# A mixer in another order: conv gate and value first, early low-priority taps, second queries ahead of attention

## The chip, the cores and the metric

The kernel runs on one core of one Trainium2 chip. The metric is the device time of one execution in microseconds (us). The core has five engines with a queue each: TensorE (PE in the profile), VectorE (DVE), ScalarE (ACT), GpSimd (POOL) and SyncE (SP), which issues nearly all transfers. Each engine takes its instructions strictly in the order in which they were put into its queue.

## The reference

Two layers of a diffusion backbone work on 640 tokens (512 latent, 128 context) of width 1024. A layer is a half-step feed-forward block, a mixer, and a second half-step feed-forward block. The change is in the mixer:

```python
h = _rms(x, p['norm_g'][1]) * (1.0 + sc2) + sh2
u = h @ p['w_in']                                   # 1536 columns: pool 256, conv 512, q 512, k 128, v 128
o_pool = _pool_mixer(u[..., :POOL_WIDTH], p['pool_w'], p['pool_scale'])
o_conv = _conv_mixer(u[..., POOL_WIDTH:ATTN_OFFSET], ...)
q, k, v = _qkv(u[..., ATTN_OFFSET:], p['q_norm_g'], p['k_norm_g'])
o_attn = ...            # 8 query heads, 2 key heads; banded latent attention plus cached context keys
x = x + g2 * (jnp.concatenate([o_pool, o_conv, o_attn], axis=-1) @ p['w_out'])

def _conv_mixer(g, dw, db, norm_g, pw):
    glu = g[..., :CONV_WIDTH] * jax.nn.sigmoid(g[..., CONV_WIDTH:])
    y = depthwise_conv(glu, dw, 31 taps, centred) + db
    return jax.nn.silu(_rms(y, norm_g)) @ pw
```

Queries and keys are normalised by head, latent ones are rotated by position (`rope`), and the softmax has a sink logit for each head.

## The kernel before, in words

Features lie on the 128 partitions and the 640 tokens along the free axis, in two halves of 320, one PSUM bank each. Products are done in fp32 by splitting both sides into a high and a low part and adding three products. A chunk of 128 output columns with 8 input blocks is 48 products of 128x128 by 320, and its weights are split by ScalarE (high) and VectorE (remainder, line 359).

`mixer` (line 784) builds the middle of a layer. `u_chunks` (line 796) makes two such chunks of the input projection for each of six names: `cg` (gate of the convolution), `ca` (its value), `kv` (keys and values), `q0` and `q1` (queries 0, 1 and 2, 3: each "query" tile holds two heads), and `pl` (pooling). `conv_gate` and `conv_value` make the gated input `glu`, one padded row of 688 for each of two channel blocks ("channels"). `conv_taps` (line 920) adds the 31 taps into `cy` (in the profile `cy<-glu,taps,cy` and `cy<-cy,cm`): those of channel 0 on VectorE (line 930); of channel 1 the first tap (line 928) and the last four on VectorE, and taps 1 to 26 as a product `cm` on ScalarE (line 933) and an add on GpSimd (line 934). The tag of these tiles has three buffers, two of which are the sums `cy`, so there is one `cm` at a time. `keys` (line 835) and `query_heads` (line 937) take the statistics of the heads, a Newton inverse root in short 128x10 steps on VectorE (lines 309 to 315), the rotation, whose two products are on GpSimd (lines 819 and 820), and the high and remainder copies `KS`, `KC` and `QS`.

Attention runs in 8 batches (`batch`, line 1057): for each of four query tiles the latent blocks 0 and 1, then 2, 3 and the context block. A batch is scores `a_*s` on TensorE, a masked maximum on VectorE (line 1083), short steps that end in `nm`, exponentials on ScalarE (line 1091), normalising copies (line 1095), transposes `a_*t` on TensorE through one PSUM bank, copies out of it on ScalarE (line 1099), and the product with the values, `a_*o` (line 1105). In the names, `a_3_2` is query tile 3, the batch that begins with block 2.

The output projection is done in two parts of four input blocks each. Part 0 (`out_chunks`, line 1111, products `p_0_m`, 24 for each of eight `m`) takes pooling and the first two attention tiles (`mix` 0, 1, 4, 5); part 1 (`last_group`, line 722, products `p_1_m_h` on line 743) takes the last two attention tiles and the convolution, and runs on into the next feed-forward block, whose row sums (`r_ss`, line 443) follow it.

What sets the order: the code states the work in one order, and a scheduler puts it on the engines' queues by priority, which follows the stated order; `high_priority(offset)` moves a piece forward (attention batches by 200) or, with a negative offset, back. The attention loop has 20 steps; tables say how much else is stated in each: `TAP_PLAN` the taps of each channel, `FILL` the modulation steps of the next block, `PLAN` the pieces of `background()` (`q1`, `pl`, then part 0), and `CONV_AT` the step from which the convolution's norm, gate and pointwise product (`convolution`) are stated. Tiles live in tagged pools; a new tile waits until the buffer it gets is read for the last time.

## Time and profile before

| | |
|---|---|
| median of 3 runs | 2480.34 us (2479.79 to 2483.69) |
| the profiled execution | 2478.26 us, span 2476.5 us |
| TensorE, VectorE, ScalarE, GpSimd busy | 95%, 69%, 41%, 19% of the span |
| first mixer | about 517 to 796 us |
| second mixer | about 1725 to 2007 us |

The page gives averages over a program in which feed-forward blocks take most of the time. The mixer is read from the busy times of single stretches and from the timeline of each engine. A timeline row is start, duration, engine, line, operation, output and inputs, shape and count; brackets at its end hold the engine's idle time before it and what ended it.

### The profile page before, as it was taken

Reading aid. Unit: us, or ns where it says so; the run is one execution under the profiler, and the core shown is the slowest. Engines: PE = TensorE matmul, PEld = TensorE weight load, DVE = VectorE, ACT = ScalarE, POOL = GpSimd, SP = SyncE. Lnnn points to the kernel's source line nnn. Section 1 sums busy time; section 2 is a strip of 40 time slices with the busy share of each in tenths; the row PEclk is TensorE's granted clock in tenths of the full one; section 3 lists DMA queues with packets and bytes.
Section 4 is the critical chain, followed back from the end, with each engine's and each line's share of the span. In section 5 each row is a group of like instructions: output and inputs, shape, how many; then the busy total and the mean of one; then the engine's idle time right before and its main releaser. Section 6 shows DMA issues by size and latency. Waiting matters only on the chain.

```text
span 2476.5 us, 40450 instructions
## 1 busy us (share of the span) xinstructions
PE 2348.3 (95%) x16491; PEld 2222.1 (90%) x16491; DVE 1707.3 (69%) x3174; ACT 1021.5 (41%) x1865; POOL 475.7 (19%) x376
## 2 busy tenths in 40 slices
PE   4999999999888899999989999999988889999999
PEld 4899999998568899999989999999975789999998
DVE  4667676667875876676669484858588569585855
ACT  2433333344674533333345242425266545242423
POOL 2101020121431211111132020212024323020210
PEclk7999999999998999999999999999998899999999
DMA  5444332222512123342312424223243022222222
GB/s 172 131 141 132 98 125 69 92 94 91 181 63 71 49 94 128 104 133 94 121 61 82 141 82 141 86 86 101 73 148 134 22 77 69 86 82 81 86 77 77
DMA packets 193990, 246.04 MB, mean 99 GB/s; under 512 B 5705, under 2 KB 176494, under 8 KB 193804
## 3 DMA queue, kind: packets, MB, share of 16 engines
q1 hardware_dynamic: 191824, 240.81, 29.9%
q8 instruction: 130, 2.13, 0.4%
q0 software_dynamic: 512, 1.95, 0.3%
q10 hardware_dynamic: 1468, 0.70, 0.1%
q14 instruction: 56, 0.46, 0.1%
HBM read 240.55 MB, written 2.88 MB: 98 GB/s over the span
## 4 chain that ended last, share of the span: by engine, by line
PE 82%; DVE 10%; ACT 4%; DMA 2%; issue 2%; SPq 0%; POOL 0%; ACTq 0%; DVEq 0%; POOLq 0%
PE f_B L555 11%; PE o_a L379 11%; PE f_C L555 11%; PE o_b L379 11%; PE f_A L555 11%; PE f_D L555 6%; PE f L596 3%; PE p L743 2%; PE mod L266 2%; PE o L743 1%; PE u_q_b L379 1%; PE u_q_a L379 1%; DVE cy L930 1%; DVE xa_l L397 1%; DVE X L421 1%
## 5 line engine op out<-in xcount | busy, mean ns | idle before, releaser
L379 PE MATMUL o_a<-f_h,o_wh 128*128 128x320 f32 x1344 | 402.9, 310 | 0.0
L379 PE MATMUL o_b<-f_h,o_wh 128*128 128x320 f32 x1344 | 401.4, 309 | 0.0
L421 DVE SCALAR_TENSOR_TENSOR X<-o_a,gate,X 128x320 f32<-128x320 f32 x120 | 65.8, 549 | 305.3 <-PE o_a L379 305.0
L379 PEld LDWEIGHTS o_a<-f_h,o_wh 128*128 128x128 f32 x1344 | 251.0, 188 | 8.7 <-ACT o_wh L358 5.8
L547 POOL TENSOR_TENSOR f_t<-f 128x512 f32<-128x512 f32 x80 | 127.6, 1595 | 660.1 <-DMA f<-in_ffn_wi_dram 556.0
L379 PEld LDWEIGHTS o_b<-f_h,o_wh 128*128 128x128 f32 x1344 | 251.4, 188 | 2.9 <-issue 2.9
L358 ACT ACTIVATE o_wh<-wo 128x768 fp32r<-128x768 f32 (+1 forms) x120 | 95.9, 800 | 381.0 <-PE o_b L379 259.7
L654 POOL TENSOR_TENSOR f_t<-f_t,f 128x512 f32<-128x512 f32 x80 | 114.4, 1430 | 638.1 <-DVE f_q_wl L533 332.8
L379 PE MATMUL o_b<-f_h,o_wl 128*128 128x320 f32 x672 | 207.3, 308 | 0.0
L379 PE MATMUL o_a<-f_h,o_wl 128*128 128x320 f32 x672 | 207.0, 308 | 0.0
L531 ACT ACTIVATE f_q_wh<-f_t 128x512 fp32r<-128x512 f32 x140 | 85.9, 629 | 199.5 <-DVE f_t L545 55.0
L379 PEld LDWEIGHTS o_b<-f_h,o_wl 128*128 128x128 f32 x672 | 126.2, 188 | 0.0
L379 PEld LDWEIGHTS o_a<-f_h,o_wl 128*128 128x128 f32 x672 | 126.0, 188 | 0.0
L359 DVE TENSOR_TENSOR o_wl<-wo,o_wh 128x768 fp32r<-128x768 f32 (+1 forms) x120 | 108.2, 903 | 15.6 <-ACT o_wh L358 15.0
L934 POOL TENSOR_TENSOR cy<-cy,cm 128x655 f32<-128x655 f32 x52 | 88.7, 1705 | 148.4 <-ACT cm L933 148.4
L531 ACT ACTIVATE f_P_wh<-f 128x512 fp32r<-128x512 f32 x112 | 66.5, 626 | 120.2 <-PE f_A L555 78.2
L555 PE MATMUL f_B<-F_h,f_q_wl 128*128 128x320 f32 x352 | 108.7, 309 | 0.8 <-DVE f_q_wl L533 0.8
L555 PE MATMUL f_B<-F_h,f_q_wh 128*128 128x320 f32 x352 | 108.7, 309 | 0.2 <-ACT f_q_wh L531 0.2
L555 PE MATMUL f_B<-F_l,f_q_wh 128*128 128x320 f32 x352 | 108.6, 308 | 0.0
L555 PE MATMUL f_C<-F_h,f_m_wh 128*128 128x320 f32 x336 | 103.6, 308 | 0.0
L555 PE MATMUL f_C<-F_l,f_m_wh 128*128 128x320 f32 x336 | 103.6, 308 | 0.0
L555 PE MATMUL f_C<-F_h,f_m_wl 128*128 128x320 f32 x336 | 103.5, 308 | 0.0
(541 smaller groups left out, 7349.9 us busy)
## 6 DMA issues: line engine op xcount, KB each, us to landing
f<-in_ffn_wi_dram SPq DMA_DIRECT2D x88, 1024.0 KB, 5.2
mw<-in_mod_w_dram SPq DMA_DIRECT2D x72, 1024.0 KB, 5.1
wo<-in_ffn_wo_dram SPq DMA_DIRECT2D x48, 768.0 KB, 4.9
wo<-in_ffn_wo_dram SPq DMA_DIRECT2D x16, 512.0 KB, 3.4
wout<-in_w_out_dram SPq DMA_DIRECT2D x32, 256.0 KB, 3.2
win_q<-in_w_in_dram SPq DMA_DIRECT2D x4, 1024.0 KB, 5.1
xt<-in_x_sample_dram SPq DMA_DIRECT2D x4, 512.0 KB, 5.5
win_cg<-in_w_in_dram SPq DMA_DIRECT2D x2, 1024.0 KB, 5.1
```

The source lines that it names most:

```text
L266: PE.matmul(ps[32 * g:32 * g + 32, 0:256], C[:, k, :], w[:, :, g, :], start=(k == 0), stop=(k == KD - 1))
L358: A.activation(out=wh, in_=src, func=AF.Copy)
L359: V.tensor_tensor(out=wl, in0=src, in1=wh.bitcast(F32), op=ALU.subtract)
L379: PE.matmul(ps[:, :n], ww[:, k, :], xx[:, lo:lo + n], start=(k == order[0] and i == 0), stop=(k == order[-1] and i == 2))
L421: V.scalar_tensor_tensor(out=X[:, m, s:e], in0=ps[:, s - o:e - o], scalar=gate[:, m, c:c + 1], in1=X[:, m, s:e], op0=ALU.mult, op1=ALU.add)
L531: A.activation(out=h, in_=src, func=AF.Copy, scale=sign)
L547: G.tensor_tensor(out=t3, in0=self.block(g, 1, 1), in1=self.block(g, 0, 1), op=ALU.add)
L555: PE.matmul(ps[:, :HALF], w[:, kp, :], self.F[f][kp][:, i, :], start=(first and kp == 0 and n == 0), stop=(kp == 3 and n == 2), skip_group ...
L596: PE.matmul(ps[:, :HALF], w[:, k, :], x, start=(k == 0 and n == 0), stop=(k == KD - 1 and n == 2))
L654: G.tensor_tensor(out=t2, in0=t2, in1=self.block(g, 1, 0), op=ALU.add)
L743: PE.matmul(ps[:, :HALF], w[:, m % 2, k, :], x[:, h * HALF:(h + 1) * HALF], start=(k == 0 and n == 0), stop=(k == 3 and n == 2))
L934: G.tensor_tensor(out=y, in0=y, in1=m, op=ALU.add)
```

## The change

The input projection is stated in the order gate, value, keys and values, queries 0, 1, and queries 2, 3 now follow ahead of the attention loop. Three taps of each channel are stated after each chunk of keys and values and of the queries, with a priority 250 lower than where they stand. In the loop each step has two taps of each channel, the convolution's norm begins at step 6 instead of 15, and `PLAN` is another. Part 0 of the output projection takes pooling and convolution, part 1 the four attention tiles. The normalised input `xa` gets a pool of its own, which is given up once the last chunk of the input projection has been stated; in its place stands a pool for tiles of pooling and convolution (two `mixp`, ten `part`) that were in the shared tags before.

```diff
-CONV_AT = 15
-TAP_PLAN = ((3, 2, 1, 2, 3, 2, 0, 2, 2, 1, 3, 2, 0, 2, 1, 3, 1, 1, 1, 3), (2, 4, 3, 3, 4, 4, 4, 2, 0, 4, 1, 1, 0, 1, 2, 1, 2, 0, 1, 4))
-ORDER, BEHIND = ("cg", "kv", "q0", "ca"), ("q1", "pl")
-PLAN = (0, 1, 0, 1, 0, 2, 0, 1, 0, 0, 0, 1, 1, 1, 2, 1, 1, 1, 1, 0)
+CONV_AT = 6
+TAP_EARLY, TAP_LATER = 3, 250
+TAP_PLAN = 2
+ORDER, BEHIND = ("cg", "ca", "kv", "q0"), ("q1", "pl")
+PLAN = (0, 1, 0, 1, 0, 1, 1, 0, 0, 0, 0, 0, 1, 1, 1, 1, 1, 1, 1, 1)
...
     def phase(name):
 
+        upper(None)
         if "cm" in scope:
...
+    def upper(name):
+
+        if "upper_cm" in scope:
+            scope.pop("upper_cm").__exit__(None, None, None)
+        if name:
+            cm = tc.tile_pool(name=name, bufs=1, reuse_waits="tile")
+            scope["upper_cm"], scope["upper"] = cm, cm.__enter__()
...
             catch_up()
+            upper(f"parts{l}")
             for c, (ph, pl) in enumerate(parts):
...
-                m = act([P, 2, T], F32R, f"mixp{l}{c}")
+                m = scope["upper"].tile([P, 2, T], F32R, tag="mixp", name=f"mixp{l}{c}", bufs=2)
...
+        def part(name, dt=F32R):
+            return scope["upper"].tile([P, T], dt, tag="part", name=name, bufs=10)
...
-                th = tmp(f"cth{l}{c}")
+                th = part(f"cth{l}{c}", F32)
...
-                mh, ml = tmp(f"mch{l}{c}", dt=F32R), tmp(f"mcl{l}{c}", dt=F32R)
+                mh, ml = part(f"mch{l}{c}"), part(f"mcl{l}{c}")
...
+        def early_taps():
+            with tc.high_priority(offset=-TAP_LATER):
+                for cc in range(2):
+                    conv_taps(cc, TAP_EARLY)
+
...
                 if k_steps and nm != "kv":
                     next(k_steps[0], None)
+                if nm in ("kv", "q0"):
+                    early_taps()
...
-            yield from out_chunks([0, 1, 4, 5], 0, lambda m: None)
+            yield from out_chunks([0, 1, 2, 3], 0, lambda m: None)
 
         bg = background()
+        for _ in range(2):
+            next(bg)
+            early_taps()
...
-                        conv_taps(cc, TAP_PLAN[cc][i], behind[cc])
+                        conv_taps(cc, TAP_PLAN, behind[cc])
...
-        for _ in conv:
-            next(bg, None)
+        assert next(conv, None) is None
...
-            for i, k in ((0, 6), (2, 2)):
+            for i, k in ((0, 4), (2, 6)):
...
-        return into_ffn(l, 2, ins["ffn2_wi"][l], f"p{l}_1", load, lambda k: mix[(6, 7, 2, 3)[k]], gate_of(l, 1, 1.0))
+        return into_ffn(l, 2, ins["ffn2_wi"][l], f"p{l}_1", load, lambda k: mix[4 + k], gate_of(l, 1, 1.0))
```

Three places in the resulting order. The first is VectorE's queue at the start of the keys' inverse root (`kv`, `rk_y` and `rk_w` are its 128x10 tiles, `u_kv_t` keys or values, `cy` the sum of channel 0, `u_q` the queries), before:

```order
L809 TENSOR_SCALAR u_kv_t<-u_kv_t,u_kv_b 128x128
L843 TENSOR_SCALAR kv_5495<-k_st 128x10
L309 TENSOR_SCALAR rk_y<-kv_5495 128x10
L312 TENSOR_TENSOR rk_w_5499<-rk_y 128x10
L313 SCALAR_TENSOR_TENSOR rk_w_5499<-rk_w_5499,kv_5495 128x10
L315 SCALAR_TENSOR_TENSOR rk_y_5502<-rk_w_5499,rk_y 128x10
L312 TENSOR_TENSOR rk_w_5504<-rk_y_5502 128x10
L313 SCALAR_TENSOR_TENSOR rk_w_5504<-rk_w_5504,kv_5495 128x10
```

and now:

```order
L940 SCALAR_TENSOR_TENSOR cy_5234<-glu_5427,taps,cy_5234 128x655 x3
L853 TENSOR_SCALAR kv_5652<-k_st 128x10
L940 SCALAR_TENSOR_TENSOR cy_5234<-glu_5427,taps,cy_5234 128x655
L319 TENSOR_SCALAR rk_y<-kv_5652 128x10
L940 SCALAR_TENSOR_TENSOR cy_5234<-glu_5427,taps,cy_5234 128x655
L322 TENSOR_TENSOR rk_w_5656<-rk_y 128x10
L425 TENSOR_TENSOR u_q_t<-u_q_a,r_5223 128x320
L323 SCALAR_TENSOR_TENSOR rk_w_5656<-rk_w_5656,kv_5652 128x10
L369 TENSOR_TENSOR u_q_wl<-win_q_5961,u_q_wh 128x1024
L325 SCALAR_TENSOR_TENSOR rk_y_5659<-rk_w_5656,rk_y 128x10
```

Taps of channel 0 and pieces of the queries' work stand ahead of and among the short steps, which followed one another before.

The second is GpSimd's queue at the first rotations (`qr_sh` and `u_q_t` of the queries, `kr_sh` and `u_kv_t` of the keys), before:

```order
L405 TENSOR_TENSOR xa_acc<-xa_acc,sq_7_5190 128x640
L819 TENSOR_TENSOR qr_sh<-qr_sh,tab_4900 128x512
L820 TENSOR_TENSOR u_q_t<-u_q_t,tab_4900 128x512
L819 TENSOR_TENSOR kr_sh<-kr_sh,tab_4900 128x512
L820 TENSOR_TENSOR u_kv_t<-u_kv_t,tab_4900 128x512
L907 MEMSET glu_5841 128x15 x3
```

and now (`cy_5235` is the sum of channel 1):

```order
L944 TENSOR_TENSOR cy_5235<-cy_5235,cm_5912 128x655
L944 TENSOR_TENSOR cy_5235<-cy_5235,cm_5915 128x655
L944 TENSOR_TENSOR cy_5235<-cy_5235,cm_6025 128x655
L829 TENSOR_TENSOR qr_sh<-qr_sh,tab_4903 128x512
L830 TENSOR_TENSOR u_q_t<-u_q_t,tab_4903 128x512
L944 TENSOR_TENSOR cy_5235<-cy_5235,cm_6028 128x655
L829 TENSOR_TENSOR kr_sh<-kr_sh,tab_4903 128x512
L830 TENSOR_TENSOR u_kv_t<-u_kv_t,tab_4903 128x512
L944 TENSOR_TENSOR cy_5235<-cy_5235,cm_6031 128x655
```

The rotations, which stood behind the squares of the norm, now stand behind and among adds of channel 1. Twelve such adds are ahead of the first rotation, 17 ahead of attention.

The third is TensorE's queue at the end of the last attention batch (`a_3_2t` its transposes, `a_3_2o` the product with the values, `rc_ss` the row sum of the convolution's norm), before:

```order
L1098 MATMUL a_3_2t_7507<-con,a_3_2S_7467 128x128 x4
L1098 MATMUL a_3_2t_7514<-con,a_3_2S_7472 128x128 x4
L1098 MATMUL a_3_2t_7521<-con,a_3_2S_7477 128x128 x3
L1098 MATMUL a_3_2t_7527<-con,a_3_2S_7482 128x128 x3
L1098 MATMUL a_3_2t_7533<-con,a_3_2S_7487 128x128
L1098 MATMUL a_3_2t_7537<-con,a_3_2S_7492 128x128
L323 MATMUL rc_ss<-ones,ca_7359 128x1 x5
L1105 MATMUL a_3_2o<-a_3_2S_7467,VS_5227 64x128
```

and now:

```order
L753 MATMUL p_1_0_0_7741<-mixa_6607,p_1_0_wh 128x320 x2
L753 MATMUL p_1_0_0_7741<-mixa_6607,p_1_0_wl 128x320
L753 MATMUL p_1_0_0_7741<-mixa_6977,p_1_0_wh 128x320 x2
L753 MATMUL p_1_0_0_7741<-mixa_6977,p_1_0_wl 128x320
L1112 MATMUL a_3_2t_7590<-con,a_3_2S_7545 128x128
L1119 MATMUL a_3_2o<-a_3_2S_7540,VS_5230 64x128
L753 MATMUL p_1_2_0_7782<-mixa_6148,p_1_2_wh 128x320 x2
L753 MATMUL p_1_2_0_7782<-mixa_6148,p_1_2_wl 128x320
```

Between the last transposes stand products of part 1 with the three attention tiles that are done (`mixa_6148`, `mixa_6607`, `mixa_6977`), and the convolution's row sum is no longer there. What stands in queues is the same in both layers.

## Rows read from the trace of the kernel before

**Rows 1.** Page: busy us (share of the span) and instructions of each engine.

```profile
PE 2348.3 (95%) x16491; PEld 2222.1 (90%) x16491; DVE 1707.3 (69%) x3174; ACT 1021.5 (41%) x1865; POOL 475.7 (19%) x376
```

**Rows 2.** Stretches: busy us and instructions by engine, granted clock, DMA share and GB/s.

```profile
core 0: us, PE busy (x) PEld busy (x) DVE busy (x) ACT busy (x) POOL busy (x), PEclk, DMA share, GB/s
516.70:603.00 86.30, 83.64 (x554) 77.89 (x553) 57.37 (x140) 29.00 (x50) 11.82 (x15) 0.96 0.27 90
540.00:603.00 63.00, 62.06 (x436) 57.27 (x435) 42.72 (x110) 21.82 (x40) 8.40 (x12) 1.00 0.26 89
603.00:737.40 134.40, 115.82 (x851) 86.21 (x849) 110.18 (x247) 91.22 (x197) 52.75 (x39) 0.94 0.35 120
737.40:795.60 58.20, 49.47 (x312) 44.08 (x312) 30.07 (x71) 30.19 (x65) 13.30 (x12) 0.85 0.23 73
741.00:765.00 24.00, 16.00 (x97) 12.05 (x97) 9.49 (x28) 12.16 (x26) 6.42 (x5) 0.66 0.07 23
1724.80:1815.70 90.90, 88.02 (x576) 81.20 (x575) 58.20 (x142) 28.96 (x49) 11.29 (x15) 0.96 0.28 96
1815.70:1948.60 132.90, 115.69 (x828) 86.26 (x827) 109.61 (x244) 91.57 (x197) 53.31 (x39) 0.88 0.33 114
1948.60:2007.20 58.60, 50.62 (x313) 44.71 (x312) 30.23 (x71) 30.21 (x65) 13.30 (x12) 0.83 0.23 73
```

**Rows 3.** Taps in X: busy us, mean ns; idle us before them and its releaser.

```profile
L934 POOL TENSOR_TENSOR cy<-cy,cm 128x655 f32<-128x655 f32 x22 | 38.3, 1742 | 64.5 <-ACT cm L933 64.5
L930 DVE SCALAR_TENSOR_TENSOR cy<-glu,taps,cy 128x655 f32<-128x655 f32 x30 | 30.9, 1029 | 0.3
L933 ACT ACTIVATE cm<-glu,taps 128x655 f32<-128x655 f32 x23 | 19.2, 835 | 3.3 <-POOL cy L934 3.3
```

**Rows 4.** Timeline of VectorE: start us, duration us, line, operation, tiles, shapes, [idle before].

```profile
559.15 0.17 DVE L312 TENSOR_TENSOR rk_w<-rk_y 128x10 f32<-128x10 f32 x1
...
579.28 1.20 DVE L312 TENSOR_TENSOR rq_w<-rq_y 128x10 f32<-128x10 f32 x1
...
583.14 0.82 DVE L955 TENSOR_TENSOR QS<-qt,QS 64x640 fp32r<-64x640 f32 x1
...
676.36 1.81 DVE L955 TENSOR_TENSOR QS<-qt,QS 64x640 fp32r<-64x640 f32 x1
```

**Rows 5.** Timeline of GpSimd beside the steps of group 4, and in the tap train.

```profile
579.18 1.29 POOL L819 TENSOR_TENSOR kr_sh<-kr_sh,tab 128x512 f32<-128x512 f32 x1
...
676.21 1.28 POOL L981 TENSOR_TENSOR pa<-pb 128x657 f32<-128x657 f32 x1
...
747.56 1.57 POOL L934 TENSOR_TENSOR cy<-cy,cm 128x655 f32<-128x655 f32 x1 [3.11 <-ACT cm L933]
750.08 1.57 POOL L934 TENSOR_TENSOR cy<-cy,cm 128x655 f32<-128x655 f32 x1 [0.95 <-ACT cm L933]
```

**Rows 6.** Timeline of ScalarE: first and last batch's exponential, two tap products.

```profile
602.97 0.71 ACT L1091 ACTIVATE a_0S<-a_0S,a_0nm,rqp 128x384 f32<-128x384 f32 x1 [2.69 <-DVE a_0nm L1087]
...
737.39 0.80 ACT L1091 ACTIVATE a_2S<-a_2S,a_2nm,rqp 128x512 f32<-128x512 f32 x1
...
746.65 0.83 ACT L933 ACTIVATE cm<-glu,taps 128x655 f32<-128x655 f32 x1
...
749.16 0.84 ACT L933 ACTIVATE cm<-glu,taps 128x655 f32<-128x655 f32 x1 [0.61 <-POOL cy L934]
```

**Rows 7.** Timeline of TensorE: the marks of S and E, transposes in E.

```profile
516.79 0.31 PE L379 MATMUL u_cg_a<-xa_h,u_cg_wh 128*128 128x320 f32 x1
...
743.20 0.66 PE L1098 MATMUL a_0t<-con,a_0S 128*128 128x128 f32 x4 [1.92 <-ACT a_0S L1099]
...
746.80 1.11 PE L1098 MATMUL a_0t<-con,a_0S 128*128 128x128 f32 x4 [2.15 <-ACT a_0S L1099]
...
752.30 0.66 PE L1098 MATMUL a_2t<-con,a_2S 128*128 128x128 f32 x4 [0.69 <-ACT a_2S L1099]
...
795.61 0.28 PE L443 MATMUL r_ss<-ones,acc 128*128 128x1 f32 x2
```

**Rows 8.** Chain of work in E: start us, us, engine, tile, line, instructions.

```profile
780.36 15.41 PE p L743 x105
```

More of the change, by code (lines that the diff above doesn't have):

```diff
@@ L383, in new_xa @@
     def new_xa(name):
-        return tuple(scope["pool"].tile([P, KD, T + 2], F32R, tag="xa", name=f"{name}_{t}", bufs=2) for t in "hl")
+        return tuple(scope["upper"].tile([P, KD, T + 2], F32R, tag="xa", name=f"{name}_{t}", bufs=2) for t in "hl")
     def shift_cols(xa, l, j, ks=slice(0, KD)):
@@ L1026, in convolution @@
             yield
-            RC = rstd_spread(dg, tmp(f"RC{l}"), bank_pair(f"rc{l}"))
+            RC = rstd_spread(dg, part(f"RC{l}", F32), bank_pair(f"rc{l}"))
             cw_raw = wpool.tile([P, 2, 256], F32, tag="raw", name=f"cpw{l}", padded_shape=[P, KD, 256], bufs=BUFS["raw"])
@@ L1038, in convolution @@
                 V.tensor_scalar(out=hg, in0=vec[:, 56 + 2 * l + c:57 + 2 * l + c], scalar1=0.5, scalar2=None, op0=ALU.mult)
-                th = tmp(f"cth{l}{c}")
+                th = part(f"cth{l}{c}", F32)
                 A.activation(out=th, in_=z, func=AF.Tanh, scale=hg)
                 V.scalar_tensor_tensor(out=z, in0=th, scalar=1.0, in1=z, op0=ALU.add, op1=ALU.mult)
-                hh, hl = tmp(f"ch{l}{c}", dt=F32R), tmp(f"cl{l}{c}", dt=F32R)
+                hh, hl = part(f"ch{l}{c}"), part(f"cl{l}{c}")
                 A.activation(out=hh, in_=z, func=AF.Copy, scale=hg)
@@ L1244, in after1 @@
                 phase(f"mix{l}")
+                upper(f"xa{l}")
                 st["a"], st["xa"], st["acc"] = prepare(l, 1, f"xa{l}1")
```

## The prediction, on record before the changed kernel ran

> **What bounds the kernel now.** I read the page's engine totals first [rows 1]: TensorE is busy 95% of the span, VectorE 69%, ScalarE 41%, GpSimd 19%. An average like this hides the stage that the change touches, so the next view is the busy time of each engine in stretches of the two mixers [rows 2]. I cut each mixer at three events: its first gate product (516.79), the first exponential of the first attention batch (602.97), the first exponential of the last batch (737.39), and the first row sum of the second feed-forward block (795.61) [rows 6, 7]. I call the three stretches S, X and E. In the first layer they are 86.30, 134.40 and 58.20 us, together 278.9; in the second 90.90, 132.90 and 58.60 [rows 2].
>
> The reader is to see three different limits. In S TensorE works 83.64 of 86.30 us and VectorE 57.37: TensorE bounds, and VectorE has 28.93 us over, 20.28 of them in the last 63 us (63.00 − 42.72) [rows 2]. In X VectorE is the busiest, 110.18 of 134.40 us (82%), ScalarE 91.22 (68%), and TensorE 115.82 at a granted clock of 0.94 [rows 2]: attention goes through VectorE and ScalarE, and TensorE fills its waits with other products. In E the span is 58.20 with TensorE busy 49.47; the bad part is 741 to 765, where TensorE is busy 16.00 of 24.00 at a granted clock of 0.66, so partly on the lower of its two levels [rows 2]. The timeline there shows transposes waiting 1.92 and 2.15 us each for ScalarE's copy that frees their one bank, and four of them taking 1.11 us where later ones take 0.66 [rows 7].
>
> **The change part by part.** Arithmetic, product counts and DMA issues stay. The order of instructions, the same in both layers, says what moves; every price below is from the trace.
>
> *Early taps and second queries in S.* Up to the last small step of the first batch's maximum (the tile whose name ends in nm), VectorE has 137 instructions of the mixer before and 184 after: 18 taps of channel 0, one start of channel 1, and 28 others (second-query head work and pooling weights). A tap is 1029 ns [rows 3], so 18 are 18.5 us. The others I price at the mean of S, 57.37 us over 140 instructions = 0.41 us, so 11.5. Together 30 us. What hides them is VectorE's idle time: 20.28 us in the last 63, but the taps need the value half of the gate, which is there after three of the eight input chunks ahead of attention (each 48 of 384 products), so I let them use 18. Spill: 30 − 18 = +12.
>
> *The GpSimd adds in S.* Of channel 1's taps, 17 are now ahead of attention; before there were none. A tap there is a ScalarE product (835 ns) and a GpSimd add (1742 ns) [rows 3]. The add doesn't run free beside VectorE. A 10-column operation of VectorE takes 0.17 us alone and 1.20 when it starts 0.10 us behind the start of a GpSimd rotation (579.18, 1.29 us) and the first 64x640 remainder takes 1.81 where another took 0.82, beside GpSimd's pooling sum at 676.21 [rows 4, 5]. Both pairs say about 1.0 us lost for each GpSimd instruction that meets VectorE at work. The loss needs VectorE to be working; at X's busy share of 0.82 it is 0.8. With 17 adds the loss is 13.6 (0.8 each) to 17 (1.0 each); I take 15. So S gets 12 + 15 = +27. Ends: +10 (all 20 us of idle time used, no collision) and +37 (10 us of it used, 17 collisions of 1.0). A gain is excluded, because TensorE's products in S stay 384 and fill 83.64 of 86.30 us now.
>
> The wait this adds: in the order shown, 12 adds stand ahead of the rotation of queries 0 and more among the next ones (17 ahead of attention), and VectorE's key chain has taps between its short steps. There is one buffer for the ScalarE product, so product and add alternate: adds start at 747.56 and 750.08, 2.52 us apart, with the second product waiting 0.61 us for the add [rows 5, 6]. Behind the rotation wait the remainders, the first scores and then all of attention. I keep that delay inside the +27, since VectorE's queue and this one run at the same time.
>
> The Trainium skill, "SBUF — State Buffer", section "Who interferes with whom", speaks against this part: a VectorE instruction with two inputs in SBUF and a GpSimd instruction that reads SBUF exclude one another for the whole instruction, and whoever comes second stands still. The trace agrees in the one pair where both ends can be read, since the 10-column step ended with the rotation (580.48 against 580.47). By the rule at its full length every add would cost VectorE up to its 1742 ns, 29.6 us for 17 instead of my 15; that result is the first rival.
>
> *The same work leaving X.* Between the nm steps of the first and of the last batch VectorE has 243 instructions before and 213 after: 32 taps become 17, and 15 others go. 15 taps × 1.029 = 15.4; the others at X's mean without taps, (110.18 − 32.9) / 215 = 0.36, are 5.4. Together −21. GpSimd adds there fall from 22 to 9: 13 × 0.8 = −10. Sum −31 on the busiest engine. ScalarE falls by 13 products × 0.835 = 11 us, from 91 to 80, while VectorE would come to 79: they are then level, so I give 2 back and take −29. Ends: −12 (X is as long as the ScalarE chain of the batches lets it be, so only ScalarE's own saving counts) and −38 (X shrinks with VectorE's work, 134.40 × 31 / 110.18).
>
> *The tail E.* Before, the convolution's norm chain and the last head's transposes stand in E with nothing between them. After, the norm and pointwise products are inside attention, all of part 0 of the output projection stands among the last batches' transposes, and part 1 begins with the three finished heads, its products between the last transposes. TensorE's 8.0 us of waiting in 741–765 can go, and four transposes again cost 0.66 instead of 1.11. Against that, X no longer has part 0 as filler, so a larger piece is left for E: one output chunk is 24 products of 0.147 us (15.41 / 105 [rows 8]), 3.5 us. Two chunks more in E give back 7. Ends −6 and +6; I take −3, as the removed wait is seen and the number of chunks left over is not.
>
> *Buffers.* The moved tiles of pooling and convolution get ten of their own in the space of the normalised input. No row shows a wait for the old ones in the convolution part (the idle time ahead of the taps is 0.3 us on VectorE [rows 3]), so I price this at 0; its ends lie within the ±6 of E.
>
> **Sum.** 27 − 29 − 3 = −5 us in a layer, −10 for two. The profiled execution took 2478.26 us with a span of 2476.5; −10 gives 2468.3. The median of the runs is 2480.34, 2.1 above it, so the forecast is 2470. My own range for this case is ±6 in a layer, 2458 to 2482.
>
> **The rivals.**
> *A: GpSimd's adds hold up the key and query chains (slower).* Each of the 17 adds stops VectorE for its whole 1742 ns in S, where every VectorE step is on the way to the first scores: 12 + 29.6 = +41 or so. X can't give all of that back, as ScalarE's 80 us and the chain of a batch stay: −29; E 0. That is +12 in a layer, 2504. It decides as soon as S grows by more than 32 (29 + 3). For it: both pairs of rows 4 and 5, and the product-add pace of 2.52 us. Against it: VectorE's mean tap among 22 adds is 1029 ns, not much above a tap's plain length, so most adds don't meet it at full length. The rule of the Trainium skill, "SBUF — State Buffer", section "Who interferes with whom", would give this time.
> *B: TensorE gets too little to do in the middle (about no change).* Part 0 is no longer there to fill attention. Where TensorE is down to 16 of 24 us now, the granted clock is 0.66 [rows 2]. The 16.00 busy us are 10.6 at full rate, so such a stretch costs 5.4. One more of it in a layer, some 6 us, makes −5 into +1: 2482. For it: the granted clock of X is already 0.94 and 0.88 [rows 2]. Against it: modulation products are still spread over attention.
> *C: attention free of collisions (much faster).* VectorE's taps and GpSimd's adds leave X almost wholly, X shrinks by 37, S grows by 20 because the adds mostly meet VectorE idle, E −2: −19 in a layer, 2442. For it: X's two ends above. Against it: 9 adds and 17 taps remain in X.
> *The change does nothing* is excluded by the order.
>
> **How the numbers follow.** Forecast 0.40, A 0.27, B 0.18, C 0.15. 0.2%, which is what a measurement of this kernel can tell from no change, is 5 us. Of the forecast's 0.40 about 0.31 lies below 2475 and 0.08 within 5 us; B is split about 0.10 same, 0.08 slower; C is faster, A slower. Together 0.46 faster, 0.18 same, 0.36 slower. The range reaches to the times of C and A, 2442 to 2504, which leaves half of each outside, 0.21.
>
> **What would show it.** Right: S near 113 us, X near 105, E near 55 in the first layer, with VectorE over 90% busy in the second half of S and rotations on GpSimd standing behind adds. A is shown by S above 118 with two-input VectorE operations of 1.5 us and more beside adds; B by a granted clock in X below 0.85; C by S under 107 with X under 100. The forecast is wrong in its mechanism if X does not shrink by at least 12 us, since then VectorE did not bound it.

## The result

The changed kernel takes 2504.56 us (median of 4 runs, 2502.11 to 2507.91) against 2480.07 us (2476.77 to 2483.69): a ratio of 1.0106, interval 1.0094 to 1.0118. It is slower by 24 us; the forecast was 10 us faster. In the table of experiments below, one execution of e13 and one of e14, which ran at a granted clock near 0.55 and took over 3700 us, are left out of the medians.

The page says little: the engine totals hardly differ from [rows 1].

```profile
PE 2351.2 (94%) x16491; PEld 2225.9 (89%) x16491; DVE 1718.2 (69%) x3174; ACT 1023.7 (41%) x1865; POOL 486.5 (19%) x376
```

The stretches S, X and E, cut at the same events as in [rows 2], tell more. Of the changed kernel, first layer and then second:

```profile
514.90:647.90 133.00, 105.11 (x658) 97.45 (x657) 104.80 (x189) 48.63 (x75) 45.37 (x38) 0.86 0.22 74
647.90:756.50 108.60, 93.92 (x665) 63.33 (x665) 78.21 (x215) 79.93 (x183) 31.44 (x22) 0.86 0.37 124
756.50:814.00 57.50, 57.50 (x409) 53.96 (x408) 25.47 (x57) 24.42 (x54) 5.28 (x6) 1.00 0.26 84
...
1740.70:1868.80 128.10, 106.72 (x670) 98.81 (x671) 102.60 (x189) 48.62 (x75) 45.90 (x38) 0.87 0.23 77
1868.80:1976.00 107.20, 90.25 (x660) 61.86 (x651) 78.17 (x215) 79.32 (x183) 30.02 (x22) 0.89 0.37 126
1976.00:2033.90 57.90, 57.90 (x407) 53.91 (x406) 25.50 (x57) 24.39 (x54) 5.28 (x6) 1.00 0.26 83
```

S grew by 46.8 and 37.2 us, X fell by 25.8 and 25.7, E by 0.7 and 0.9. The mixers are 20.3 and 10.6 us longer; what lies around them is 7.1 us shorter (2500.3 − 2476.5 = 23.8). The reader is to see TensorE's two columns. In S it has 104 more instructions (658 against 554) and 27.9 us of idle time (133.00 − 105.11) against 2.7; in X 186 fewer (665 against 851); in E 97 more and no idle time at all. By the names of the tiles in the first layer, 115 products of the output projection left X, and E has 129 more of them; 94 of the input projection and 10 for the statistics of the queries went from X to S; 38 of the convolution came from E into X. The granted clock of X fell from 0.94 to 0.86 there and stayed in the second layer (0.88 and 0.89).

Where the idle time in S comes from is shown by TensorE's waits there (us in total, times, longest):

```profile
PE u_q_b L389 <- DVE u_q_t L426: 13.7, 1, 13.7
PE qst L823 <- ACT qsq L950: 6.0, 3, 4.8
PE mod L276 <- DMA mw<-in_mod_w_dram: 5.3, 1, 5.3
```

The largest is one wait: TensorE can't begin the next query chunk until VectorE has read the last one out of its PSUM bank. The wait, VectorE's queue at that place, and GpSimd's:

```profile
589.17 0.61 PE L389 MATMUL u_q_b<-xa_h,u_q_wh 128*128 128x322 f32 x1 [13.73 <-DVE u_q_t L426]
```

```profile
574.58 5.27 DVE L940 SCALAR_TENSOR_TENSOR cy<-glu,taps,cy 128x655 f32<-128x655 f32 x3
...
579.89 0.90 DVE L940 SCALAR_TENSOR_TENSOR cy<-glu,taps,cy 128x655 f32<-128x655 f32 x1
580.71 1.54 DVE L319 TENSOR_SCALAR rk_y<-kv 128x10 int32<-128x10 int32 x1
...
585.81 1.52 DVE L325 SCALAR_TENSOR_TENSOR rk_y<-rk_w,rk_y 128x10 f32<-128x10 f32 x1
...
588.54 0.48 DVE L426 TENSOR_TENSOR u_q_t<-u_q_b,r 128x320 f32<-128x320 f32 x1
```

```profile
574.40 1.71 POOL L944 TENSOR_TENSOR cy<-cy,cm 128x655 f32<-128x655 f32 x1 [0.95 <-ACT cm L943]
...
577.06 2.10 POOL L944 TENSOR_TENSOR cy<-cy,cm 128x655 f32<-128x655 f32 x1 [0.70 <-ACT cm L943]
580.11 2.10 POOL L944 TENSOR_TENSOR cy<-cy,cm 128x655 f32<-128x655 f32 x1 [0.95 <-ACT cm L943]
583.16 1.56 POOL L944 TENSOR_TENSOR cy<-cy,cm 128x655 f32<-128x655 f32 x1 [0.95 <-ACT cm L943]
585.68 1.63 POOL L944 TENSOR_TENSOR cy<-cy,cm 128x655 f32<-128x655 f32 x1 [0.95 <-ACT cm L943]
...
604.94 1.26 POOL L829 TENSOR_TENSOR qr_sh<-qr_sh,tab 128x512 f32<-128x512 f32 x1 [2.18 <-DVE qr_sh L828]
```

Three taps beside adds take 5.27 us together, 1.76 each, and one between adds 0.90; 10-column steps take 1.54 and 1.52 instead of 0.17; and the adds themselves 2.10 instead of 1.56. Taps, key steps and adds push the bank's read to 588.54, and TensorE starts at 589.17. The first rotation, 604.94, didn't wait behind the adds ahead of it: GpSimd had stood idle for 2.18 us, until VectorE's shuffle was there. The same holds for the rotations of the later queries in both layers (idle 2.18 to 8.19 us and 3.01 and 6.47), so the forecast's wait of a rotation behind a train of adds is not what happened.

### The profile page after: what moved, and what is told of

Same layout as the page of the kernel before. It is cut to its first block, busy times and chain, and to the rows that moved or that the text cites. A ratio compares the mean times of both kernels' runs of the same rounds, so it can differ in the third digit from the quotient of the medians.

```text
span 2500.3 us, 40465 instructions
## 1 busy us (share of the span) xinstructions
PE 2351.2 (94%) x16491; PEld 2225.9 (89%) x16491; DVE 1718.2 (69%) x3174; ACT 1023.7 (41%) x1865; POOL 486.5 (19%) x376
## 4 chain that ended last, share of the span: by engine, by line
PE 81%; DVE 11%; ACT 3%; DMA 2%; issue 1%; POOL 0%; SPq 0%; ACTq 0%; DVEq 0%
PE f_B L565 11%; PE f_C L565 11%; PE o_a L389 11%; PE f_A L565 11%; PE o_b L389 11%; PE f_D L565 6%; PE f L606 3%; PE p L753 2%; DVE cy L940 2%; PE mod L276 2%; PE p_a L389 1%; PE p_b L389 1%; PE o L753 1%; DMA mw<-in_mod_w_dram 1%; DVE xa_l L407 1%
## 5 line engine op out<-in xcount | busy, mean ns | idle before, releaser
L368 ACT ACTIVATE o_wh<-wo 128x768 fp32r<-128x768 f32 (+1 forms) x120 | 95.9, 801 | 379.4 <-PE o_b L389 262.0
L565 PE MATMUL f_C<-F_h,f_m_wh 128*128 128x320 f32 x336 | 103.8, 309 | 0.0
L565 PE MATMUL f_C<-F_l,f_m_wh 128*128 128x320 f32 x336 | 103.8, 309 | 0.0
```

The source lines that it names most:

```text
L368: A.activation(out=wh, in_=src, func=AF.Copy)
L565: PE.matmul(ps[:, :HALF], w[:, kp, :], self.F[f][kp][:, i, :], start=(first and kp == 0 and n == 0), stop=(kp == 3 and n == 2), skip_group ...
```

## The experiments

A table of stretches, read from each kernel's trace at the same marks (in the kernels that begin with keys and values, S begins with their first product). Each is of one execution, the profiled one, which lies within 5 us of its kernel's median. Ratios are to runs of the kernel before beside it, with 95% intervals.

| kernel | median us | ratio | S | X | E |
|---|---|---|---|---|---|
| before | 2480.07 | 1 | 86.2, 90.9 | 134.4, 132.9 | 58.2, 58.8 |
| changed | 2504.56 | 1.0106 [1.0094, 1.0118] | 133.0, 128.1 | 108.6, 107.2 | 57.5, 57.9 |
| e1 no early taps | 2569.76 | 1.0367 [1.0351, 1.0383] | 114.3, 113.0 | 153.5, 148.6 | 66.6, 63.2 |
| e2 early taps of channel 0 only | 2559.13 | 1.0328 [1.0313, 1.0344] | 115.0, 113.2 | 139.4, 142.5 | 67.7, 67.1 |
| e3 second queries in the loop | 2505.55 | 1.0107 [1.0090, 1.0124] | 103.8, 104.2 | 129.5, 129.9 | 63.8, 61.7 |
| e4 before, new order only | 2491.10 | 1.0051 [1.0035, 1.0066] | 98.1, 99.3 | 131.2, 134.5 | 56.9, 57.9 |
| e5 neither early taps nor second queries | 2552.28 | 1.0299 [1.0284, 1.0315] | 95.9, 97.3 | 159.8, 157.7 | 63.9, 63.8 |
| e6 early taps of channel 1 only | 2497.86 | 1.0083 [1.0068, 1.0098] | 120.7, 123.5 | 109.2, 112.4 | 58.0, 63.1 |
| e7 before, chains first | 2465.14 | 0.9945 [0.9930, 0.9960] | 76.9, 83.2 | 134.7, 141.0 | 58.2, 51.1 |
| e8 before, new order, early taps | 2483.65 | 1.0024 [1.0014, 1.0033] | 104.6, 104.8 | 127.0, 127.4 | 49.9, 50.6 |
| e9 before, second queries ahead | 2487.68 | 1.0040 [1.0026, 1.0054] | 101.6, 97.2 | 126.6, 124.4 | 58.2, 62.2 |
| e10 changed, chains first | 2493.91 | 1.0067 [1.0052, 1.0082] | 107.3, 107.6 | 124.2, 119.0 | 64.6, 58.0 |
| e11 before, all chains first | 2475.72 | 0.9993 [0.9984, 1.0003] | 97.9, 90.0 | 123.9, 131.7 | 58.9, 54.6 |
| e12 e7, 20 GpSimd taps | 2455.93 | 0.9911 [0.9896, 0.9926] | 78.6, 83.2 | 138.6, 139.1 | 50.1, 51.1 |
| e13 changed, early taps on VectorE | 2495.85 | 1.0065 [1.0045, 1.0084] | 125.1, 125.3 | 101.3, 107.1 | 58.0, 62.5 |
| e14 e7, 14 GpSimd taps | 2448.77 | 0.9882 [0.9860, 0.9904] | 78.4, 83.2 | 139.6, 136.8 | 46.3, 46.0 |
| e15 e10, 14 GpSimd taps | 2477.62 | 0.9997 [0.9987, 1.0006] | 110.0, 107.4 | 119.4, 116.0 | 57.5, 57.5 |

### Taking the pieces out: e1, e3, e5, e4

```diff
-TAP_EARLY, TAP_LATER = 3, 250        # e1, e5
-TAP_PLAN = 2
+TAP_EARLY, TAP_LATER = 0, 250
+TAP_PLAN = 4                         # e5: 5; e3: 3 with TAP_EARLY = 3
...
-        for _ in range(2):            # e3, e5
-            next(bg)
-            early_taps()
-PLAN = (0, 1, 0, 1, 0, 1, 1, 0, 0, 0, 0, 0, 1, 1, 1, 1, 1, 1, 1, 1)     # e3, e5
+PLAN = (0, 1, 0, 1, 0, 2, 0, 1, 1, 0, 0, 0, 1, 1, 1, 1, 1, 1, 1, 1)
...
-ORDER, BEHIND = ("cg", "kv", "q0", "ca"), ("q1", "pl")     # e4, in the kernel before
+ORDER, BEHIND = ("cg", "ca", "kv", "q0"), ("q1", "pl")
```

> The changed kernel without early taps (0 instead of 3 after each chunk; four taps of each channel in each loop step until step 6, where the rest is stated). Second queries stay ahead of attention. Theory T (taps in front of the key and query chains, with the collisions of GpSimd's adds, cost the time): S falls by 25 us or more in each layer, X grows by about 12, so 2478 us or less. Theory Q (the second queries ahead of attention cost it: their 96 products, and the first batch's maximum standing behind their chain on VectorE): S falls by under 12 us, X grows by as much, 2497 to 2507 us.

> The changed kernel with the second queries back in the attention loop (steps 1 and 3, as before the change), early taps only after keys, values and first queries (12 of each channel instead of 18), three taps a step in the loop. Theory Q: the wait of the first maximum behind the second queries' chain goes and their products come back as filler, S falls by 25 us in each layer and X grows by about 12: about 2478 us. Theory T: two thirds of the early taps are still in front of the chains, S falls by 10 to 15 and X grows by as much: 2495 to 2507 us.

> The changed kernel with neither early taps nor second queries ahead (five taps a step in the loop until step 6; second queries at steps 1 and 3). What stays of the change: gate and value first, convolution from step 6, parts of the output projection, buffers. If T and Q each hold a part of the loss and add up, this is the fastest of the four, about 2470 us, with S within 8 us of the 86 and 91 us of before. If the loss sits in what stays (theory R: tail, buffers or gate and value first), it is still 2495 us or more.

> The kernel before with one line of the change: the input projection in the order gate, value, keys and values, first queries. Theories T and Q: key and query chains end some 14 us later in S with no product left behind them, so S grows by 5 to 12 us in each layer and X keeps its length or loses a few: 2480 to 2500 us. Theory R in its form that this order alone costs the loss: 2500 us or more.

e1 misses both ranges and is far slower, by a wait that I had not thought of. e5 is over R's bound of 2495 us, but with the same wait (23.1 us), which no theory named. e3 has the time that T gave, but not by T's terms: S fell by 29.2 and 23.9 us where T had 10 to 15, and X grew by 20.9 and 22.7 and E by 6.3 and 3.8, so that second queries and six taps in the loop or ahead of it come to the same. Of e1, TensorE's waits in X:

```profile
PE rc_ss L333 <- POOL ca L1037: 25.6, 1, 25.6
PE a_2s L1094 <- DVE a_2mx L1097: 14.6, 5, 7.9
```

The convolution's row sum stands in TensorE's queue early, since the convolution is stated at step 6; it waits 25.6 us for GpSimd's train of channel 1, and attention waits behind it. So with the convolution at step 6 the early taps are needed, and the times of e1 and e5 don't price them. Their S does, since it ends before that wait. From before over e5 and e1 to the changed kernel S grows in three steps, which add up by construction: the order (with what else stays in e5) 9.7 and 6.4 us, the second queries ahead 18.4 and 15.7, the early taps 18.7 and 15.1. The prices depend on what stands beside them: with the second queries in the loop, twelve early taps of each channel cost 7.9 and 6.9 (e3 against e5), and in the old order the second queries ahead cost 15.4 and 6.3 (e9). e4 confirms the first step: order alone gives S +11.9 and +8.4, and 13 us in all (2491.10 against 2478.19 in the runs beside it). S of e4, first layer:

```profile
516.10:614.20 98.10, 90.76 (x585) 84.28 (x585) 60.83 (x144) 30.91 (x51) 12.50 (x16) 0.90 0.29 101
```

The chains end later: 31 more instructions of TensorE stand before the first exponential, its idle time grows from 2.7 to 7.3 us (waits for a transfer of modulation weights, 3.3, and for squares of the queries from ScalarE, 2.3), and the clock falls from 0.96 to 0.90.

Of e5 and e1, S of the first layer. The second queries bring 73 instructions of TensorE (a pooling chunk of 48 products is among them), and 14.8 of the 18.4 us are TensorE's busy time (103.33 − 88.56):

```profile
516.50:612.40 95.90, 88.56 (x586) 82.13 (x585) 60.81 (x144) 30.92 (x51) 12.53 (x16) 0.93 0.30 103
```

```profile
515.00:629.30 114.30, 103.33 (x659) 95.70 (x657) 70.55 (x170) 35.38 (x59) 16.35 (x21) 0.91 0.26 86
```

### What makes the early taps dear: e2, e6, e13

```diff
-                for cc in range(2):
-                    conv_taps(cc, TAP_EARLY)
+                conv_taps(0, TAP_EARLY)        # e2; e6: conv_taps(1, TAP_EARLY)
...
-                        conv_taps(cc, TAP_PLAN, behind[cc])
+                        conv_taps(cc, (2, 4)[cc], behind[cc])        # e6: (4, 2)[cc]
...
-                    elif c == 0 or tp > POOL_TAPS:                      # e13 alone
+                    elif c == 0 or tp < 18 or tp > POOL_TAPS:
```

> The changed kernel with early taps of channel 0 (VectorE) alone; channel 1's are stated four a step in the loop. Read by stretch. Without any early tap S was 114.3 and 113.0 us, with both channels 133.0 and 128.1. Theory G (GpSimd's adds, their collisions with VectorE and the rotations behind them, make these 17 us): S is 114 to 120 here. Theory V (the 18 taps on VectorE itself make them, by their own length): S is 126 to 133. X will be long in both, about 150 us, as GpSimd's train then holds the convolution's row sum on TensorE as without early taps; in all 2550 us or more.

> The changed kernel with early taps of channel 1 (ScalarE product, GpSimd add) alone; channel 0's are stated four a step in the loop. Theory G: S stays at 126 to 133 us. Theory V: S falls to 114 to 120. In both X gets the 18 taps of channel 0 back, 18.5 us of VectorE's time, and is 115 to 127 instead of 108. In all 2500 to 2530 us by G, 2485 to 2500 by V.

> The changed kernel with taps 1 to 17 of channel 1, the early ones, on VectorE instead of ScalarE and GpSimd; taps 18 to 26 stay on GpSimd in the loop. VectorE gets 17 x 0.9 = 15 us more in S, and no GpSimd add stands there. Theory G (collisions of adds with VectorE make the early taps dear): the collisions' loss in S goes and 15 us come; S is 115 to 130 us and TensorE's stall ahead of u_q_b is under 10 us; 2480 to 2500 us. Theory V (any VectorE work in front of the chains is paid in full): S is 140 us or more, the stall over 13.7 us, 2510 us or more.

S of the first layer in e2, e6 and e13:

```profile
515.90:630.80 114.90, 102.49 (x658) 95.14 (x657) 84.26 (x189) 35.08 (x58) 15.21 (x21) 0.91 0.25 86
```

```profile
517.90:638.60 120.70, 104.03 (x659) 96.53 (x657) 85.94 (x171) 48.78 (x76) 44.56 (x38) 0.89 0.24 82
```

```profile
518.20:643.20 125.00, 102.67 (x658) 95.66 (x657) 97.06 (x206) 35.20 (x58) 15.21 (x21) 0.88 0.23 79
```

VectorE's 18 taps alone cost nothing (S +0.7 and +0.2 against e1): VectorE's busy time rises from 70.55 to 84.26 and all of it is hidden. GpSimd's 17 adds alone cost 6.4 and 10.5, and VectorE's busy time rises by 15.4 us although only one tap came, 0.9 us for each add. Together VectorE is busy 104.80, and S is 18.7 longer. e13, with 17 more taps of VectorE's own (12.8 us more than e2) and no add, is busy 97.06, and S is 8 and 3 us shorter than in the changed kernel. Neither theory holds as stated: V fails in e2, and in e6 S lies between the two. VectorE's busy time with collisions counted in goes with S: up to some 84 us it is hidden; from there to 104.8 (20.5 us more) S grows by 18. But it isn't the whole: e6 has only 1.7 us more of it than e2, and S is 5.8 longer, 10.2 in the other layer. There the adds stop the short key steps right ahead of the bank's read, five of them for 1.42 to 1.53 us instead of 0.17. The first of them and the read in e6, then the read in e2:

```profile
573.95 1.51 DVE L319 TENSOR_SCALAR rk_y<-kv 128x10 int32<-128x10 int32 x1
...
582.82 0.48 DVE L426 TENSOR_TENSOR u_q_t<-u_q_b,r 128x320 f32<-128x320 f32 x1
```

```profile
576.51 0.48 DVE L426 TENSOR_TENSOR u_q_t<-u_q_b,r 128x320 f32<-128x320 f32 x1
```

So what stands ahead of that read counts, whether taps or stopped steps. TensorE's wait ahead of `u_q_b` in the first layer's S follows it: absent in e1, 2.3 us in e2, 6.5 in e6, 12.2 in e13 (I had said under 10), 13.7 in the changed kernel. Of the 8 us of S between these last two, 1.5 are of this wait, 4.1 of others and 2.4 of TensorE's busy time.

### Is X bound by VectorE? e6, e8, e9

```diff
+        bg = background()                     # e9, in the kernel before
+        for _ in range(2):
+            next(bg)
-PLAN = (0, 1, 0, 1, 0, 2, 0, 1, 0, 0, 0, 1, 1, 1, 2, 1, 1, 1, 1, 0)
+PLAN = (0, 1, 0, 1, 0, 0, 0, 1, 0, 0, 0, 1, 1, 1, 2, 1, 1, 1, 1, 0)
...
+                if nm in ("kv", "q0"):        # e8, in the kernel of e4
+                    early_taps()
```

> The kernel before with the new order and three early taps of each channel after each chunk of keys, values and first queries (12 of each channel); convolution from step 15, parts of the output projection, second queries in the loop and buffers as before the change. With the new order alone it was 2491.1 us, S 98.1, X 131.2, E 56.9 in the first layer. Theory B (VectorE bounds X, so work that leaves it comes back): X falls by 20 us (12 x 1.03 + 12 x 0.8 = 22), S grows by 10, 2472 us. Theory L (X is as long as the chain of the batches, and the earlier convolution is what shortened it in the changed kernel): X falls by under 8, S grows by 10, 2495 us.

> The kernel before with the second queries' two steps ahead of the attention loop (pooling then at steps 1 and 3); all else as before. Theory L (TensorE's ledger: the time of the mixer is its products plus the idle time that the order makes, so products moved from X to S are paid in S and saved in X): S grows by 14 to 20 us, X falls by 14 to 20, 2470 to 2486 us. Theory B (VectorE bounds X, as the forecast had it): the second queries' VectorE work leaves X as well, X falls by 25 or more, S grows by 12, 2455 us or less. Theory Q: the first maximum waits behind the second queries' chain and nothing pays for it, 2490 us or more.

e6 answers it first. X of e6, first layer:

```profile
638.60:747.70 109.10, 85.87 (x657) 56.98 (x656) 93.56 (x230) 77.56 (x179) 31.23 (x22) 0.91 0.33 119
```

VectorE works 15.4 us more than in the changed kernel's X (93.56 against 78.21), and X is 0.5 us longer in this layer, 5.2 in the other, where I had expected 7 to 19. In e8 it works 16 us less than in e4, and X is 4.2 and 7.1 us shorter: theory L's figure, and 24 and 27 products of the output projection (3.5 and 4.0 us at 0.147) went from X to E. But e8 is 2483.65, not 2495, because S grew by 6.5 and 5.5 us, where both theories had 10, and E fell by 7, which neither had. E of e8, first layer:

```profile
748.30:798.20 49.90, 48.63 (x344) 44.26 (x344) 27.84 (x70) 27.96 (x61) 5.25 (x6) 1.00 0.26 85
```

TensorE is idle for 1.3 us there against 8.5 in e4, and no add of channel 1 is left in E, where e4 has three; that the convolution's norm is no longer late for this reason is likely, but wasn't tried by itself. In e9 S grew by 15.4 and 6.3, X fell by 7.8 and 8.5; the total, 2487.68, lies between the ranges of L and Q. The second queries ahead cost 10 us by themselves (2487.68 against 2477.76 beside it): S takes 21.7 us in the two layers, X gives back 16.3, and E of the second layer takes 3.4. X of e9, first layer:

```profile
622.30:748.90 126.60, 107.77 (x761) 75.74 (x760) 94.05 (x217) 85.58 (x187) 47.67 (x33) 0.85 0.34 119
```

It has 90 instructions of TensorE fewer than before, 13.2 us at 0.147, and gives back only 7.8: the idle time stays (18.8 us against 18.6), and the granted clock is 0.85 instead of 0.94, so what is left takes longer.

### Chains first: e7, e10, e11, e12, e14, e15

```diff
-ORDER, BEHIND = ("cg", "kv", "q0", "ca"), ("q1", "pl")
+ORDER, BEHIND = ("kv", "q0", "cg", "ca"), ("q1", "pl")     # e7, e12, e14; e10 and e15 in the changed kernel
...
-POOL_TAPS = 26
+POOL_TAPS = 20                        # e12; e14 and e15: 14
...
-ORDER, BEHIND = ("cg", "kv", "q0", "ca"), ("q1", "pl")
-PLAN = (0, 1, 0, 1, 0, 2, 0, 1, 0, 0, 0, 1, 1, 1, 2, 1, 1, 1, 1, 0)
+ORDER, BEHIND = ("kv", "q0", "q1", "cg", "ca"), ("pl",)    # e11
+PLAN = (0, 0, 0, 0, 0, 2, 0, 1, 0, 0, 0, 1, 1, 1, 2, 1, 1, 1, 1, 0)
...
-TAP_EARLY, TAP_LATER = 3, 250
+TAP_EARLY, TAP_LATER = 6, 250         # e10, e15
...
-                if nm in ("kv", "q0"):
-                    early_taps()
+            if nm == "ca":             # e10, e15
+                early_taps()
```

> The kernel before with the input projection in the order keys and values, first queries, gate, value: the opposite move to the order of the change. Theory C (the key and query chains need 96 or more products behind them as cover; moving the value ahead of them took that cover away and cost 8 to 12 us in S): with 192 products behind, the first exponential comes 8 to 14 us earlier after the first product of the input projection; the products move into X, where VectorE bounds, so the whole gains 3 to 8 us in a layer, 2464 to 2474 us. Rival: the cover was complete before, the first exponential gains nothing by it and the taps start later: 2478 to 2495 us.

> The kernel with keys, values and first queries first, then gate and value (2465.1 us; X 134.7 and 141.0, E 58.2 and 51.1), with 20 instead of 26 taps of channel 1 on GpSimd; the other six go to VectorE. Theory L: VectorE has idle time in X, so X stays within 3 us, and GpSimd's shorter train lets the convolution's norm come earlier, E of the first layer falls by 4 to 8: 2453 to 2463 us. Theory B: six taps more on the engine that bounds X, X grows by 6 in each layer, 2470 us or more.

> The kernel with keys, values and first queries first, 14 taps of channel 1 on GpSimd instead of 20 (2455.9 us) or 26 (2465.1). Theory L: VectorE's work in X is hidden until it is as long as X; it goes from 114 to about 119 of 139 us, so X stays and fewer adds slow VectorE: 2448 to 2457 us. Theory B: X grows by 5 us in each layer, 2462 us or more.

> The kernel before with the input projection in the order keys and values, first and second queries, gate, value. Theory L: 96 products go from X to S against the kernel with keys, values and first queries first (2465.1 us), and the cover stays; within 6 us of that one, 2459 to 2471. Theory B: 2450 us or less, as VectorE's work of the second queries leaves X. Rival: the taps start later and GpSimd's train holds the tail, 2475 us or more.

> The changed kernel with the chains first: order keys and values, first queries, gate, value; early taps six of each channel after the value and after each step of the second queries (18 of each in all, as in the change). Theory C (the loss in S is keys and queries without cover, behind taps and adds): S falls from 133 and 128 to 100 to 112, X and E stay within 8 us, 2445 to 2475 us. Rival G2 (adds and taps collide with the chains wherever they stand in S): S stays above 120, 2490 us or more.

> The changed kernel with the chains first and six early taps of each channel after the value and the second queries' steps (2493.9 us; S 107, X 124 and 119, E 65 and 58), with 14 instead of 26 taps of channel 1 on GpSimd. If GpSimd's train is what lengthened X there (its adds beside VectorE's steps of the batches), X falls to 112 or less: 2465 to 2480 us. If X is long there for the products and idle time of the batches themselves, it stays above 118: 2488 us or more.

e7, the opposite move to the change's, is faster than before, as theory C said. S and X of its first layer:

```profile
515.00:591.90 76.90, 74.25 (x486) 70.07 (x486) 58.56 (x139) 29.28 (x49) 11.23 (x15) 0.98 0.25 86
591.90:726.60 134.70, 119.83 (x911) 90.77 (x910) 112.41 (x247) 91.93 (x197) 53.09 (x39) 0.95 0.36 128
```

68 products fewer come before the first exponential, S is 9.3 us shorter, and X takes 60 more for 0.3 us: they fill TensorE's idle time there, 18.6 us before and 14.9 now. In the second layer it goes another way: S is 7.7 us shorter, X with 42 more 8.1 longer, and E 7.7 shorter. e12 and e14 then lengthen VectorE's work in X and shorten GpSimd's train of adds, and both come out at the time that theory L gave, though X of e12 grew by 3.9 us in the first layer, where L had 3 at most (in the other it fell by 1.9). Of e14, the first layer:

```profile
515.00:593.40 78.40, 75.78 (x487) 71.62 (x487) 58.60 (x140) 29.31 (x50) 11.21 (x15) 0.96 0.25 85
593.40:733.00 139.60, 123.02 (x962) 94.26 (x960) 120.14 (x271) 88.18 (x193) 41.08 (x33) 0.99 0.36 127
733.00:779.30 46.30, 41.49 (x267) 37.64 (x268) 22.95 (x57) 24.79 (x56) 5.28 (x6) 0.89 0.25 80
```

VectorE is busy 120.14 us of X against 112.41 in e7, X is 4.9 us longer in this layer (with 51 more products of TensorE) and 4.2 shorter in the other, and E 11.9 and 5.1 shorter. e14 is the fastest of all, 2448.77 us, 1.2% under the kernel before. e11 missed its range of 2459 to 2471 by 5 us and has the rival's time; but the tail, which the rival blamed, is not the main part: against e7, S grew by 21.0 and 6.8 us, X fell by 10.8 and 9.3, and E grew by 0.7 and 3.5. Second queries ahead cost here too.

In the changed kernel, chains first brings S to 107 us, as theory C said, and X grows to 124.2 and 119.0, which it did not; 2493.91 instead of at most 2475. e15 asks whether GpSimd's train does that. Its S is 110.0 and 107.4, X 119.4 and 116.0, E 57.5 in both, 2477.62 us: the total is in the range for "the train", X of the first layer in that for "not the train". A part of it is the train; what else holds X there, 25 us of TensorE idle, stays open. No single wait of TensorE makes it: the longest in total is 6.7 us for modulation weights, then 4.7 for squares of the queries.

## Why the prediction was wrong

S was forecast at +27 us and grew by 46.8 and 37.2. Of the 19.8 and 10.2 us too much, the order makes 9.7 and 6.4, the second queries 6.9 and 4.2 over their price, the taps and adds 3.2 and −0.4. X and E miss by 5.5 and 5.4 more.

**The order.** I priced the products of the stretches by the change's text, and the move of the value ahead of the keys and queries not at all. Alone it costs 11.9 and 8.4 us of S (e4): the value's 96 products stand ahead of the chains and no longer behind them as cover. e7, the opposite move, makes S shorter by 9.3 and 7.7. This is the first failed step, a term put at nothing.

**"TensorE's products in S stay 384".** This sentence failed most. Before, 50 (in the second layer 73) of the second queries' 96 products were ahead of the first exponential; now all of them are, with a pooling chunk of 48 and 10 more for statistics, and 104 and 94 more instructions were recorded. I had priced this piece as 28 small VectorE steps, 11.5 us, and nothing on TensorE. It costs 18.4 and 15.7, most of it TensorE's busy time. Beside this, the first scores are there long before VectorE reaches their maximum, whose place in its queue is behind the second queries' chain; what that alone costs wasn't tried. Scores on TensorE, then the first maximum on VectorE:

```profile
621.60 0.51 PE L1094 MATMUL a_0s<-KS,QS 128*128 128x384 f32 x2
```

```profile
639.28 0.54 DVE L1097 CUSTOM_DVE_ANT_0 a_0S<-a_0s,tab 128x384 f32<-128x384 f32 x1
```

**The taps and adds in S.** Right: 18.5 + 15 − 18 = +15.5 was forecast, +18.7 and +15.1 were measured, and an add cost VectorE 0.9 us where I had said 0.8 to 1.0. The taps hide, as forecast (e2); the adds cost 6.4 and 10.5 without them and 18.0 and 14.9 on top of them. The price is less than an add's whole length: over 17 adds e6 shows 15.4 us, not 29.6. Beside the first of them VectorE does nothing, and where VectorE began first the add waited (2.10 us instead of 1.56 in the changed kernel). The Trainium skill, "SBUF — State Buffer", section "Who interferes with whom", has a VectorE instruction with two inputs in SBUF and a GpSimd instruction that reads SBUF exclude one another, so that the second stands still until the first ends. The trace agrees with that for single pairs: the two-input step of 585.81 ended with the add that had begun 0.13 us before it (587.33 against 587.31).

**X.** The size was right, −29 against −25.8 and −25.7, but by luck; the reason was wrong. VectorE's busy time does not bound X (e6, e12, e14). 186 instructions of TensorE left it, 27.3 us at 0.147 [rows 8], and came back in S (104) and E (97, with a few more or fewer recorded); X's idle time fell only from 18.6 to 14.7 us. I had seen VectorE's 82% and not asked what else left with the work. The sign that I had named, that X shrinks by at least 12, can't tell the two causes apart. What sets the idle time that stays in X is open.

**E.** −3 was forecast, −0.7 and −0.9 measured. TensorE's idle time went, 8.7 us (58.20 − 49.47 in [rows 2]) to none, and the granted clock rose from 0.85 to 1.00, as forecast; but 97 instructions more came in, 14.3 us, where I had allowed 7. e8, which keeps the old parts, shows the gain with a smaller bill (24 products more than in e4): E is 49.9 and 50.6.

**Rival A** gave 2504 and has the measured time to a microsecond, but by luck and not by its mechanism: adds alone cost 6.4 and 10.5 us, not 29.6, and the rotations didn't wait for them. Its S of +41 was met by order, second queries, and taps together. Its signs, S over 118 and two-input steps of 1.5 us beside adds, were both there all the same. The granted clock in X, 0.86 and 0.89, was above B's bound of 0.85; still, it fell from 0.94 in the first layer, as B's mechanism has it.

**Around the mixers** 7.1 us went that I had not looked for. 2 to 3 us of it lie behind each mixer and recur in every kernel with the new parts of the output projection and the new buffers: 926.1 to 928.2 us from the first mixer to the second, against 929.2 to 932.1 with the old. Which of the two does it wasn't tried.

## What to carry to other kernels

Keep a ledger of the engine that does the products: for each stretch its instructions, its idle time and its clock. Work that is moved out of one stretch appears in another; only a change in idle time or clock is a gain, and a busy neighbour is no bound until more work on it makes the stretch longer. Put long chains first and the products that nobody waits for behind them. Before an engine's queue gets filler, see which of its reads of PSUM another engine waits for, and what would then stand ahead of them.

## What was not expected of the hardware

A 10-column step with one input in SBUF was held as well: 1.54 us beside an add of GpSimd, against 0.17. And what two engines' work costs alone does not add up to what it costs together: 18 taps (0.7 us of S) and 17 adds (6.4) cost 18.7 together in the first layer. They slow each other, taps from 0.90 to 1.76 us and adds from 1.56 to 2.10, and together they use up the idle time that hides either.
